# A per-channel normalisation on one core: units of twice the size, with rows of 64 KB

## The chip, the cores and the metric

The kernel runs on one core of one Trainium2 chip. The metric is the device time of one execution in microseconds; the number given for a kernel is the median of its runs. A profile comes from one further execution. Its times are counted from the start of its span, which is a little shorter than the device time.

## What is computed

```python
def setup_inputs():
    B, G, C_per_g, H, W = 4, 8, 16, 256, 256
    return {
        "x": np.random.randn(B, G, C_per_g, H, W).astype(np.float32),
        "gamma": np.random.randn(G, C_per_g).astype(np.float32),
    }

def reference(x, gamma):
    mu = x.mean(axis=(3, 4), keepdims=True)
    var = ((x - mu) ** 2).mean(axis=(3, 4), keepdims=True)
    x_norm = (x - mu) / np.sqrt(var + 1e-5)
    return x_norm * gamma[None, :, :, None, None]
```

There are 4 x 8 x 16 = 512 channels of 256 x 256 = 65,536 float32 values. Each channel is brought to mean zero and variance one, and multiplied by its gamma, of which there are 128 (one for each g and c, the same for all four b). The input is 134.2 MB, and so is the output. Each is moved once.

## The kernel before

A channel lies on 8 partitions, as 8 rows of 8192 values (32 KB). So 128 partitions hold 16 channels, and this is one unit: a tile of 128 x 8192 float32, 4 MB. There are U = 32 units. Six slots (`AHEAD`) hold them in SBUF, and unit u uses slot u % 6.

The order of the work is written out by hand. SP's queue issues the loads, except those of units 1 and 3, which ScalarE's queue issues at the start. ScalarE's queue issues all stores. Six loads are issued at once; after that the load of unit u + 6 (L48) waits until unit u has been normalised and stored, since it overwrites its slot.

For each unit:

- VectorE sums each row (`reduce_sum`, L102), and ScalarE sums the squares of each row (`Square` with `accum_out`, L103). Both read the whole tile at the same time.
- One matmul (L113) with the matrix `navg` adds up the 8 rows of each channel, for the sum and the sum of squares together, and leaves the negative means in `ps` on every row of the channel. `navg` holds -1/65536 in 8 x 8 blocks along the diagonal.
- VectorE makes the negative variance (`nvar`, L114), ScalarE its root (`std`, L118), VectorE the reciprocal (L122) and the product with gamma (`scale`, L124).
- VectorE normalises the whole tile in place (L127): add the negative mean, multiply by `scale`.
- ScalarE's queue stores the tile (L131), and SP's queue issues the load that comes into this slot next.

`g_col` holds gamma by partition, one column for each of the 8 groups of 16 channels. It is made by `gamma_columns` (L78 to L89): a copy on VectorE that repeats each gamma 8 times in one row, 8 matmuls that turn rows into columns, and a copy out of PSUM. It runs after the first unit's sums. Gamma itself comes on SP's queue, behind the load of unit 0. The table for Sqrt is loaded when the first root is due.

Of the kernel before, what the change touches and what calls it, by code (L numbers as in the profile page):

```python
# [1 line left out]

# [4 lines left out]

F32 = mybir.dt.float32
U8 = mybir.dt.uint8
ALU = mybir.AluOpType  # L10
ACTF = mybir.ActivationFunctionType
AX = mybir.AxisListType


@with_exitstack
def kernel(
    ctx: ExitStack,
    tc: tile.TileContext,
    x: bass.AP,
    gamma: bass.AP,  # L20
    out: bass.AP,
):
    nc = tc.nc
    B, G, C, H, W = x.shape
    P = nc.NUM_PARTITIONS
    HW = H * W
    n_ch = B * G * C
    S = 8
    K = P // S
    F = HW // S  # L30
    U = n_ch // K
    NG = (G * C) // K
    AHEAD = 6
    assert HW % S == 0 and (G * C) % K == 0

    xv = x.rearrange("b g c h w -> (b g c h w)").rearrange("(u p f) -> u p f", p=P, f=F)
    ov = out.rearrange("b g c h w -> (b g c h w)").rearrange("(u p f) -> u p f", p=P, f=F)
    gv = gamma.rearrange("g c -> (g c)")

    data = ctx.enter_context(tc.tile_pool(name="data", bufs=1))  # L40
    singles = ctx.enter_context(tc.tile_pool(name="singles", bufs=1))
    psum = ctx.enter_context(tc.tile_pool(name="psum", bufs=4, space=bass.MemoryType.PSUM))
    ctx.enter_context(tc.manual_schedule())

    slots = [data.tile([P, F], F32, name=f"xt{i}") for i in range(AHEAD)]

    def load(u, queue):
        queue.dma_start(out=slots[u % AHEAD][:], in_=xv[u])  # L48


    g_row = singles.tile([1, G * C], F32, name="g_row")
    for u in range(AHEAD):
        load(u, nc.scalar if u in (1, 3) else nc.sync)
        if u == 1:
            nc.sync.dma_start(out=g_row[:], in_=gv[None, :])


    eps_t = singles.tile([P, 1], F32, name="eps_t")
    nc.gpsimd.memset(eps_t[:], 1e-5)
    one = singles.tile([1, 1], F32, name="one")  # L60
    nc.gpsimd.memset(one[:], 1.0)
    navg = singles.tile([P, K, S], F32, name="navg")
    nc.gpsimd.memset(navg[:], -1.0 / HW)  # L63
    nc.gpsimd.affine_select(  # L64
        out=navg[:], in_=navg[:], pattern=[[-S, K], [0, S]], compare_op=ALU.is_ge,
        fill=0.0, base=0, channel_multiplier=1,
    )
    nc.gpsimd.affine_select(  # L68
        out=navg[:], in_=navg[:], pattern=[[S, K], [0, S]], compare_op=ALU.is_ge,
        fill=0.0, base=S - 1, channel_multiplier=-1,  # L70
    )
    navg_w = navg[:].rearrange("p k s -> p (k s)")
    g_rep = singles.tile([1, NG, K, S], F32, name="g_rep")
    g_ps = psum.tile([P, NG], F32, name="g_ps", bufs=1)
    g_col = singles.tile([P, NG], F32, name="g_col")

    def gamma_columns():
        nc.vector.tensor_copy(  # L78
            out=g_rep[:],
            in_=g_row[:].rearrange("o (n k) -> o n k", n=NG).unsqueeze(3).to_broadcast([1, NG, K, S]),  # L80
        )
        for n in range(NG):
            nc.tensor.matmul(  # L83
                out=g_ps[:, n : n + 1],
                lhsT=g_rep[:, n].rearrange("o k s -> o (k s)"),
                rhs=one[:],
                start=True, stop=True,
            )
        nc.vector.tensor_copy(out=g_col[:], in_=g_ps[:])  # L89

    junk = singles.tile([P, F], U8, name="junk")

    st = singles.tile([P, U, 2], F32, name="st")
    nvar = singles.tile([P, U], F32, name="nvar")
    std = singles.tile([P, U], F32, name="std")
    rstd = singles.tile([P, U], F32, name="rstd")
    scale = singles.tile([P, U], F32, name="scale")

    squares = []
    for u in range(U):  # L100
        t = slots[u % AHEAD]
        nc.vector.reduce_sum(out=st[:, u, 0:1], in_=t[:], axis=AX.X)  # L102
        square = nc.scalar.activation(  # L103
            out=junk[:], in_=t[:], func=ACTF.Square, accum_out=st[:, u, 1:2],
        )
        if u:

            tc.declare_no_dep(square.ins, squares[-1].ins, reason="junk, ordered by the root between")
        squares.append(square)
        if u == 0:  # L110
            gamma_columns()
        ps = psum.tile([P, 2], F32, name="ps")
        nc.tensor.matmul(out=ps[:], lhsT=navg_w, rhs=st[:, u], start=True, stop=True)  # L113
        nc.vector.tensor_scalar(  # L114
            out=nvar[:, u : u + 1], in0=ps[:, 0:1], scalar1=ps[:, 0:1],
            scalar2=ps[:, 1:2], op0=ALU.mult, op1=ALU.add,
        )
        nc.scalar.activation(  # L118
            out=std[:, u : u + 1], in_=nvar[:, u : u + 1], func=ACTF.Sqrt,
            bias=eps_t[:], scale=-1.0,  # L120
        )
        nc.vector.reciprocal(out=rstd[:, u : u + 1], in_=std[:, u : u + 1])  # L122
        g = u % NG
        nc.vector.tensor_mul(  # L124
            out=scale[:, u : u + 1], in0=rstd[:, u : u + 1], in1=g_col[:, g : g + 1],
        )
        nc.vector.tensor_scalar(  # L127
            out=t[:], in0=t[:], scalar1=ps[:, 0:1], scalar2=scale[:, u : u + 1],
            op0=ALU.add, op1=ALU.mult,
        )  # L130
        nc.scalar.dma_start(out=ov[u], in_=t[:])  # L131
        if u + AHEAD < U:
            load(u + AHEAD, nc.sync)


# [1 line left out]
_INS = ['x', 'gamma']  # L137
_OUTS = [((4, 8, 16, 256, 256), 'float32')]


# [23 lines left out]
```

## Time and profile before

| what | value |
|---|---|
| median of 9 runs | 627.1 us (626.81 to 627.25) |
| profiled execution | 627.1 us, its span 625.4 us |
| VectorE busy | 442.9 us, 71% of the span |
| ScalarE busy | 239.9 us, 38% |
| TensorE busy (matmul) | 21.4 us, 3% |
| HBM read and written | 134.22 MB each, 429 GB/s over the span |
| the queue DMA q10 (all stores and two loads) | 4896 packets, 142.61 MB, 52.8% of the 16 engines' span |
| the queue DMA q1 (30 loads and gamma) | 4322 packets, 125.83 MB, 46.8% |

The share of a queue is the time that its packets took, against the span of all 16 DMA engines; the two together fill it. SP, the queue that issues loads, waited 538.9 us in all for stores to end, in 26 waits: a load cannot be issued until the store has emptied its slot. A packet in the trace is one descriptor: here one row of 32 KB, or the 4 bytes that count up a semaphore at the end of a transfer.

### The profile page before, as it was taken

How to read it: one execution, taken by the hardware profiler on the slowest of the kernel's cores; microseconds unless marked ns; L12 is line 12 of the kernel's file. 1: busy time of each engine (PE TensorE's matmuls, PEld its weight loads, DVE VectorE, ACT ScalarE, POOL GpSimd, SP SyncE). 2: the span in 40 equal slices, each digit the busy share in tenths (PEclk: the TensorE clock that was granted, in tenths of full speed). 3: DMA queues.
4: the chain of work that ended last, by engine and by line, in shares of the span. 5: the costliest groups of instructions: out<-in, count | busy, mean ns of one | idle time of the engine just before them, and what ended most of it. 6: DMA issues, size and time to landing. Idle time of an engine off the chain costs nothing.

```text
span 625.4 us, 628 instructions
## 1 busy us (share of the span) xinstructions
PE 21.4 (3%) x80; PEld 19.5 (3%) x80; DVE 442.9 (71%) x162; ACT 239.9 (38%) x98; POOL 1.3 (0%) x9
## 2 busy tenths in 40 slices
PE   0020000000000000000000000000000000000000
PEld 0020000000000000000000000000000000000000
DVE  0569999999898667867668676686766877667710
ACT  0435555544444423444224442244432444323400
POOL 0000000000000000000000000000000000000000
DMA  8999999999999999999999999999999999999998
GB/s 369 436 434 405 436 436 436 436 436 436 434 434 428 428 428 432 436 434 436 436 436 434 436 432 432 430 430 428 436 436 434 436 436 432 436 436 434 430 425 361
DMA packets 9220, 268.46 MB, mean 429 GB/s; under 512 B 1025, under 2 KB 1026, under 8 KB 1026
## 3 DMA queue, kind: packets, MB, share of 16 engines
q10 hardware_dynamic: 4896, 142.61, 52.8%
q1 hardware_dynamic: 4322, 125.83, 46.8%
q14 instruction: 2, 0.02, 0.0%
HBM read 134.22 MB, written 134.22 MB: 429 GB/s over the span
## 4 chain that ended last, share of the span: by engine, by line
DMA 62%; DVE 30%; PE 2%; issue 1%; ACT 1%; SPq 0%; ACTq 0%
DMA xt<-in_x_dram 54%; DVE st L102 24%; DMA out_dram<-xt 7%; DVE xt L127 5%; PE ps L113 2%; DVE nvar L114 1%; PE g_ps L83 1%; ACT std L118 0%; ACT L118 0%; DVE rstd L122 0%; DVE scale L124 0%; DVE g_rep L78 0%; SPq L48 0%; ACTq L118 0%
## 5 line engine op out<-in xcount | busy, mean ns | idle before, releaser
L102 DVE TENSOR_REDUCE st<-xt 128x1 f32<-128x8192 f32 x32 | 277.9, 8684 | 110.5 <-DMA xt<-in_x_dram 110.5
L103 ACT ACTIVATE junk<-xt 128x8192 uint8<-128x8192 f32 x32 | 225.0, 7030 | 266.4 <-DMA xt<-in_x_dram 212.4
L127 DVE TENSOR_SCALAR xt<-xt,ps,scale 128x8192 f32<-128x8192 f32 x32 | 145.6, 4550 | 1.2
L118 ACT ACTIVATE std<-nvar,eps_t 128x1 f32<-128x1 f32 x32 | 9.4, 295 | 76.0 <-DVE nvar L114 76.0
L113 PE MATMUL ps<-st,navg 128*128 128x2 f32 x64 | 17.9, 349 | 536.7 <-DVE st L102 536.7
L113 PEld LDWEIGHTS ps<-st,navg 128*128 128x128 f32 x64 | 16.1, 312 | 538.4 <-issue 538.4
L114 DVE TENSOR_SCALAR nvar<-ps 128x1 f32<-128x1 f32 x32 | 9.2, 286 | 23.4 <-PE ps L113 23.4
L122 DVE RECIPROCAL rstd<-std 128x1 f32<-128x1 f32 x32 | 5.2, 164 | 12.9 <-ACT std L118 12.9
L103 ACT ACTIVATION_READ_ACCUMULATOR junk<-xt 128x1 f32 x32 | 6.0, 186 | 0.0
L124 DVE TENSOR_TENSOR scale<-rstd,g_col 128x1 f32<-128x1 f32 x32 | 5.1, 159 | 1.1
L83 PE MATMUL g_ps<-one,g_rep 1*128 1x1 f32 x16 | 3.5, 346 | 32.1 <-DVE g_rep L78 32.1
L83 PEld LDWEIGHTS g_ps<-one,g_rep 1*128 1x128 f32 x16 | 3.5, 325 | 32.0 <-issue 32.0
L118 ACT ACT_TABLE_LOAD x1 | 1.3, 1283 | 6.8 <-DVE nvar L114 6.8
L89 DVE COPY g_col<-g_ps 128x8 f32<-128x8 f32 x1 | 0.2, 167 | 3.7 <-PE g_ps L83 3.7
L103 ACT ACT_TABLE_LOAD x1 | 1.3, 1283 | 1.7 <-PEq L148 1.7
L78 DVE COPY g_rep<-g_row 1x1024 f32<-1x1024 f32 x1 | 0.7, 671 | 0.0
L64 POOL TENSOR_SCALAR_AFFINE_SELECT navg<-navg 128x128 f32<-128x128 f32 x1 | 0.4, 405 | 0.1
L68 POOL TENSOR_SCALAR_AFFINE_SELECT navg<-navg 128x128 f32<-128x128 f32 x1 | 0.4, 399 | 0.1
L63 POOL MEMSET navg<- 128x128 f32 x1 | 0.2, 222 | 0.0
L148 POOL MEMSET const-bfloat16-1.0<- 128x1 bf16 x1 | 0.1, 102 | 0.0
L148 POOL MEMSET const-uint8-127<- 128x1 uint8 x1 | 0.1, 102 | 0.0
L148 POOL MEMSET const-float32-0.0<- 128x1 f32 x1 | 0.1, 99 | 0.3 <-issue 0.3
(3 smaller groups left out, 0.3 us busy)
## 6 DMA issues: line engine op xcount, KB each, us to landing
out_dram<-xt ACTq DMA_DIRECT2D x32, 4096.0 KB, 64.4
xt<-in_x_dram SPq DMA_DIRECT2D x30, 4096.0 KB, 29.0
xt<-in_x_dram ACTq DMA_DIRECT2D x2, 4096.0 KB, 31.5
g_row<-in_gamma_dram SPq DMA_DIRECT2D x1, 0.5 KB
```

The source lines that it names most:

```text
L64: nc.gpsimd.affine_select(out=navg[:], in_=navg[:], pattern=[[-S, K], [0, S]], compare_op=ALU.is_ge, fill=0.0, base=0, channel_multiplier=1,)
L68: nc.gpsimd.affine_select(out=navg[:], in_=navg[:], pattern=[[S, K], [0, S]], compare_op=ALU.is_ge, fill=0.0, base=S - 1, channel_multipli ...
L78: nc.vector.tensor_copy(out=g_rep[:], in_=g_row[:].rearrange("o (n k) -> o n k", n=NG).unsqueeze(3).to_broadcast([1, NG, K, S]),)
L83: nc.tensor.matmul(out=g_ps[:, n : n + 1], lhsT=g_rep[:, n].rearrange("o k s -> o (k s)"), rhs=one[:], start=True, stop=True,)
L102: nc.vector.reduce_sum(out=st[:, u, 0:1], in_=t[:], axis=AX.X)
L103: square = nc.scalar.activation(out=junk[:], in_=t[:], func=ACTF.Square, accum_out=st[:, u, 1:2],)
L113: nc.tensor.matmul(out=ps[:], lhsT=navg_w, rhs=st[:, u], start=True, stop=True)
L114: nc.vector.tensor_scalar(out=nvar[:, u : u + 1], in0=ps[:, 0:1], scalar1=ps[:, 0:1], scalar2=ps[:, 1:2], op0=ALU.mult, op1=ALU.add,)
L118: nc.scalar.activation(out=std[:, u : u + 1], in_=nvar[:, u : u + 1], func=ACTF.Sqrt, bias=eps_t[:], scale=-1.0,)
L122: nc.vector.reciprocal(out=rstd[:, u : u + 1], in_=std[:, u : u + 1])
L124: nc.vector.tensor_mul(out=scale[:, u : u + 1], in0=rstd[:, u : u + 1], in1=g_col[:, g : g + 1],)
L127: nc.vector.tensor_scalar(out=t[:], in0=t[:], scalar1=ps[:, 0:1], scalar2=scale[:, u : u + 1], op0=ALU.add, op1=ALU.mult,)
```

## The change

A unit becomes 32 channels. A channel now lies on 4 partitions, as rows of 16,384 values (64 KB); a slot holds 128 x 16384 float32, 8 MB, and there are 3 of them (`SL`). V = 16 such units cover the input. In the listing, v counts units, h the two halves of a unit (16 channels, 64 rows each). Half h lies on every second partition, from partition h on (`t[h::2]`). Each half is loaded by one transfer and stored by another.

- The last unit keeps the old form: two narrow units of 16 channels, 8 partitions for each, side by side in the columns of one slot, each with its own load (L57 of the new listing; wide halves are loaded on L59) and store over all 128 partitions, and with its own sums.
- All loads are on SP's queue. Gamma comes first on ScalarE's queue. The gamma columns (two for the last two narrow units, four for the wide ones) are made ahead of all units, and a Sqrt of `eps_t`, whose result isn't used, loads the table ahead too.
- The matrix for wide units, `navg_w`, is made by GpSimd: within a block of 8 partitions, -1/65536 where the row and the column number differ by an even number. `navg_n` for the narrow ones is the old matrix.
- In a wide unit the squares come in two instructions of 8192 columns, with one accumulator each, and the matmul becomes three: one for the sum, two that add up the squares.
- VectorE normalises the first 10,240 columns (`DV`) of a wide unit. ScalarE normalises the other 6,144 with `Identity`, with `scale` and a `shift` (negative mean times `scale`), which is one more small VectorE instruction.

```diff
-    S = 8
-    AHEAD = 6
+    SL = 3
+    FW = HW // 4
+    FN = HW // 8
+    V = n_ch // 32
+    DV = 10240
+    xw = xf.rearrange("(v h r f) -> v h r f", h=2, r=P // 2, f=FW)
+    ow = of.rearrange("(v h r f) -> v h r f", h=2, r=P // 2, f=FW)
+    xn = xf.rearrange("(n p f) -> n p f", p=P, f=FN)
+    on = of.rearrange("(n p f) -> n p f", p=P, f=FN)
-    slots = [data.tile([P, F], F32, name=f"xt{i}") for i in range(AHEAD)]
-    def load(u, queue):
-        queue.dma_start(out=slots[u % AHEAD][:], in_=xv[u])
+    slots = [data.tile([P, FW], F32, name=f"xt{i}") for i in range(SL)]
+    def load_slot(v):
+        t = slots[v % SL]
+        for h in range(2):
+            if v == V - 1:
+                nc.sync.dma_start(out=t[:, h * FN : (h + 1) * FN], in_=xn[2 * v + h])
+            else:
+                nc.sync.dma_start(out=t[h::2], in_=xw[v, h])
...
-    for u in range(AHEAD):
-        load(u, nc.scalar if u in (1, 3) else nc.sync)
-        if u == 1:
-            nc.sync.dma_start(out=g_row[:], in_=gv[None, :])
+    nc.scalar.dma_start(out=g_row[:], in_=gv[None, :])
+    for v in range(SL):
+        load_slot(v)
...
+    nc.scalar.activation(out=root_eps[:], in_=eps_t[:], func=ACTF.Sqrt)
...
+    for d in (-6, -4, -2, 0, 2, 4, 6):
+        nc.gpsimd.affine_select(
+            out=navg_w[:], in_=navg_w[:], pattern=[[-8, P // 8], [-1, 8]],
+            compare_op=ALU.not_equal, fill=-1.0 / HW, base=-d, channel_multiplier=1,
+        )
+    block8(navg_w)
...
+    def unit(i, t, width, navg, g):
+        nsq = width // FN
+        nc.vector.reduce_sum(out=st[:, i, 0:1], in_=t, axis=AX.X)
+        for k in range(nsq):
+            sq = nc.scalar.activation(
+                out=junk[:], in_=t[:, k * FN : (k + 1) * FN], func=ACTF.Square,
+                accum_out=st[:, i, 1 + k : 2 + k],
+            )
...
+        if nsq == 1:
+            nc.tensor.matmul(out=ps[:], lhsT=w, rhs=st[:, i, 0:2], start=True, stop=True)
+        else:
+            nc.tensor.matmul(out=ps[:, 0:1], lhsT=w, rhs=st[:, i, 0:1], start=True, stop=True)
+            nc.tensor.matmul(out=ps[:, 1:2], lhsT=w, rhs=st[:, i, 1:2], start=True, stop=False)
+            nc.tensor.matmul(out=ps[:, 1:2], lhsT=w, rhs=st[:, i, 2:3], start=False, stop=True)
...
+        w = width
+        if nsq > 1:
+            w = DV
+            nc.vector.tensor_mul(out=shift, in0=ps[:, 0:1], in1=scale)
+            nc.scalar.activation(
+                out=t[:, w:], in_=t[:, w:], func=ACTF.Identity, bias=shift, scale=scale,
+            )
         nc.vector.tensor_scalar(
+            out=t[:, :w], in0=t[:, :w], scalar1=ps[:, 0:1], scalar2=scale,
             op0=ALU.add, op1=ALU.mult,
         )
...
+    for v in range(V):
+        t = slots[v % SL]
+        if v == V - 1:
+            for h in range(2):
+                part = t[:, h * FN : (h + 1) * FN]
+                unit(i, part, FN, navg_n, h)
+                nc.scalar.dma_start(out=on[2 * v + h], in_=part)
+                i += 1
+        else:
+            unit(i, t[:], FW, navg_w, NE + v % NW)
+            for h in range(2):
+                nc.scalar.dma_start(out=ow[v, h], in_=t[h::2])
+            i += 1
+        if v + SL < V:
+            load_slot(v + SL)
```

## The prediction

> **What bounds the kernel now.** I read the page's slices first, then its groups and DMA issues, then the timeline of the end, then the trace's packet records (one per descriptor: queue, start, duration, bytes).
>
> ```profile
> span 625.4 us, 628 instructions
> DVE  0569999999898667867668676686766877667710
> ACT  0435555544444423444224442244432444323400
> DMA  8999999999999999999999999999999999999998
> GB/s 369 436 434 405 436 436 436 436 436 436 434 434 428 428 428 432 436 434 436 436 436 434 436 432 432 430 430 428 436 436 434 436 436 432 436 436 434 430 425 361
> L102 DVE TENSOR_REDUCE st<-xt 128x1 f32<-128x8192 f32 x32 | 277.9, 8684 | 110.5 <-DMA xt<-in_x_dram 110.5
> L103 ACT ACTIVATE junk<-xt 128x8192 uint8<-128x8192 f32 x32 | 225.0, 7030 | 266.4 <-DMA xt<-in_x_dram 212.4
> L127 DVE TENSOR_SCALAR xt<-xt,ps,scale 128x8192 f32<-128x8192 f32 x32 | 145.6, 4550 | 1.2
> out_dram<-xt ACTq DMA_DIRECT2D x32, 4096.0 KB, 64.4
> xt<-in_x_dram SPq DMA_DIRECT2D x30, 4096.0 KB, 29.0
> ```
>
> The DMA row is full from end to end: the 16 DMA engines bound everything, and VectorE's 71% is not the limit. A store takes 64.4 us from issue to landing, a load 29.0: stores stand in a long queue. Now the end:
>
> ```profile
> 561.33 8.69 DVE L102 TENSOR_REDUCE st<-xt 128x1 f32<-128x8192 f32 x1 [4.34 <-DMA xt<-in_x_dram]
> 571.80 4.55 DVE L127 TENSOR_SCALAR xt<-xt,ps,scale 128x8192 f32<-128x8192 f32 x1
> 580.70 7.03 ACT L103 ACTIVATE junk<-xt 128x8192 uint8<-128x8192 f32 x1 [9.31 <-DMA xt<-in_x_dram]
> 580.70 8.69 DVE L102 TENSOR_REDUCE st<-xt 128x1 f32<-128x8192 f32 x1 [4.34 <-DMA xt<-in_x_dram]
> 591.17 4.55 DVE L127 TENSOR_SCALAR xt<-xt,ps,scale 128x8192 f32<-128x8192 f32 x1
> 595.75 0.34 ACTq L131 DMA_DIRECT2D out_dram<-xt  x1
> ```
>
> Units come every 19.37 us (580.70 less 561.33). From the last landing, reduce to store issue takes 15.05 us (580.70 to 595.75), all of it under stores queued earlier: those run to 623.9 by the packet records, and the span ends at 625.4.
>
> The records give more. First packet at 1.8 us, last end 623.9, so 622.1 us of transfer. A 32 KB packet starts 1.2097 us after the one before on its engine. Load and store packets alternate one for one, whatever the queues hold, and a transfer's 4-byte semaphore packet also takes a turn. A load's last packet ended 1.6 us before the reduce (579.11, 580.70). Issue to first packet is 1.0 us on idle engines (0.8 to 1.8), but 5.0 us for the first store (43.11 to 48.1), which enters while loads run and costs 0.9 us.
>
> [...]
>
> **The change, part by part.** The sum is on the profiled execution: 627.1 us, span 625.4 plus 1.7 around it; the median is 627.1 too.
>
> Start. The copy for gamma (0.67 us), its 16 matrix passes (3.54) and the Sqrt table (1.28) leave the stretch from 31.2 to 37.8 us and go beside the first landing (22.6 us). POOL's masks grow by some ten instructions of 0.2 to 0.4 us, done by about 7 us; the first matmul wants them near 40. Gamma is one 512-byte packet ahead on ScalarE's queue; SP now issues all early loads, six at 0.35 us, against 9.7 us of transfer each. Value of all this: 0. Loads alone fill the engines to 1.8 + 6 x 9.66 = 59.8 us, and the first store is ready at 22.7 + 25.1 = 48 (43 before). Without this cover each late microsecond would count.
>
> Compute of a wide unit: reduce 2 x 8.68 = 17.4; three matmuls, 0.7 to 1.7 (one is 0.57 with its two passes); nvar, root, reciprocal, scale 1.0 with gaps; shift 0.2 by the scale row; normalise 4.55 x 10240/8192 = 5.7. About 25.1 us against 38.6 us of DMA per unit. Beside it ScalarE does two squares, 14.4, and 6144 columns of Identity: 5.3 at Square's rate, at worst twice that. Both ends are hidden: a slot turns in 3 x 38.6 = 116 us, less load 39, landing and compute 28, first store half 19 and refill 3 to 5, leaving some 25 us in the store queue. The stores' extra waits on shared DMA semaphores (half h of unit v waits for half h of v-2, with the next squares behind it on ScalarE) end some 12 us before the issue. Cost 0.
>
> Packets. [...] Fifteen units go from 16 to 8 packets per engine each way: 240 fewer, 240 x 5 ns = **-1.2 us**. If rows were cut in two again, 0[...].
>
> The end. This decides. A wide load waits for its own half's store alone. The two narrow loads of the last unit (L57) write all 128 partitions, so both wait for both stores of unit 12, on SP with nothing behind them. So the load queue runs dry while unit 12's second store moves, and stores run ahead. Count turns from that store's end. Stores of units 13 and 14 hold 4 halves x (4 packets + 1 semaphore) = 20 turns, then the first narrow store 9. The two loads hold 18. They arrive 1.6 + 1.0 = 2.6 us later at best, 6.6 with the first store's 5.0: two or three store packets of 2.41 us are gone. The other 17 or 18 store turns pair off with the 18 load turns. But a store turn is 64 KB and a load turn 32 KB: stores get 63% of the engines. When the last load ends, units 13 and 14 are out and only the first narrow store is left: 8 x 1.21 = 9.7 us. The last half needs 1.6 landing + 15.05 + 1.0 to its first packet = 17.7. The engines stand idle 17.7 - 9.7 = **+8.0 us**. One store turn more or less gives 5.6 to 10.4; a restart stall as at the first store 0.9 on top. Before, 623.9 - 579.1 = 44.8 us remained after the last load, less 9.7 of its own store: nothing was exposed.
>
> Sum: 627.1 - 1.2 + 8.0 = 633.9, say **634.0 us**; this case's own range is 631.5 to 638.
>
> **Rivals.**
> [...]
>
> Equal shares at the end, not slower. If engines share by bytes and not by descriptors, the last loads' 19.4 us go beside 19.4 of stores. From unit 12's end 48.3 us of stores remain; head start 5 to 7, so 22 to 24 are left when the loads end, more than 17.7. No idle time: 627.1 - 1.2 = 625.9. It decides below a store share of about 56%: then at most 48.3 - 17.7 = 30.6 us of stores are gone. Against: strict alternation of records; all were of one size, so before can't tell.
>
> The change doesn't do what it says: 64 KB rows are moved as two of 32 KB. Then turns are equal, no packet is saved, no idle: 627.1. For it: before shows nothing over 32 KB.
>
> **How the numbers follow.** Forecast 0.57, collisions 0.19, cut rows 0.13, equal shares 0.11. A measurement here tells about 0.2% (1.25 us) from no change. 625.9 stands on that edge, so half of its chance is faster: 0.06. Same: 0.13 + 0.05 = 0.18. Slower: 0.57 + 0.19 = 0.76. The range leaves out the collisions: 625.5 to 638, with 0.81 inside.
>
> **What would show it.** Right: packets of 65,536 bytes at about 2.41 us; full DMA slices until some 611 us, then about 8 us without packets while one narrow reduce, chain and normalise run; the last store issued near 619; the last loads half as dense in packets' time as the stores beside them. Wrong: packets still of 32 KB; packet durations well over 2.41 us all through (collisions); no DMA gap, with over 17.7 us of stores after the last load; or idle time in the middle, which would mean the 25 us in the store queue don't exist.

## The result, and the profile after

| | median | executions | ratio, 95% interval |
|---|---|---|---|
| before | 627.1 us | 626.8 to 627.5 (29) | |
| changed | 639.4 us | 637.3 to 642.3 (9) | 1.0199 [1.0189, 1.0209] |
| forecast | 634.0 us | range 625.5 to 638.0 | |

Slower, as forecast, but by 12.3 us and not by 6.9, and past the upper end of the range by 1.4. The changed kernel also scatters over 5.0 us, the kernel before over 0.7. The profiled execution is the fastest of the nine, 637.3 us with a span of 635.4: it stands 10.2 us above the one before, and is read with that in mind.

First the page of the changed kernel: its slices, groups (busy us and mean ns of one behind the first bar) and DMA issues (the last number is the median us from issue to landing).

```profile
span 635.4 us, 657 instructions
...
DMA  9999999999999999999999999999999999999976
GB/s 396 396 462 396 458 400 458 417 441 454 408 450 409 450 421 437 454 417 446 413 446 433 429 454 417 441 421 437 450 417 447 425 433 437 410 421 406 421 309 264
DMA packets 5381, 268.47 MB, mean 422 GB/s; under 512 B 1025, under 2 KB 1026, under 8 KB 1026
...
L129 DVE TENSOR_REDUCE st<-xt 128x1 f32<-128x16384 f32 (+1 forms) x17 | 275.7, 16215 | 205.7 <-DMA xt<-in_x_dram 205.7
...
L162 DVE TENSOR_SCALAR xt<-xt,ps,cf 128x10240 f32<-128x10240 f32 (+1 forms) x17 | 93.2, 5484 | 0.1
L159 ACT ACTIVATE xt<-xt,cf 128x6144 f32<-128x6144 f32 x15 | 82.6, 5508 | 10.2 <-DVE cf L158 10.2
...
xt<-in_x_dram SPq DMA_DIRECT2D x30, 26.1
out_dram<-xt ACTq DMA_DIRECT2D x30, 45.5
```

The DMA row is as full as before in 38 slices, and thins out in the last two (309 and 264 GB/s, against 425 and 361 before). VectorE still waits 205.7 us for loads, so it is not the limit. The GB/s row swings between 396 and 462: a slice is 15.9 us, and 6 packets of 64 KB on each of 16 engines make 396 GB/s in it, 7 make 462. By itself the swing is no loss.

Next the timeline of the changed kernel's end: start, us, engine and line, and in brackets the idle time before and who ended it.

```profile
542.67 17.22 DVE L129 TENSOR_REDUCE st<-xt 128x1 f32<-128x16384 f32 x1 [13.35 <-DMA xt<-in_x_dram]
547.56 1.03 SPq L57 DMA_DIRECT2D xt<-in_x_dram  x2
...
579.31 8.69 DVE L129 TENSOR_REDUCE st<-xt 128x1 f32<-128x8192 f32 x1 [11.16 <-DMA xt<-in_x_dram]
...
594.37 0.38 ACTq L174 DMA_DIRECT2D out_dram<-xt  x1
...
608.05 8.69 DVE L129 TENSOR_REDUCE st<-xt 128x1 f32<-128x8192 f32 x1 [13.71 <-DMA xt<-in_x_dram]
...
618.52 4.55 DVE L162 TENSOR_SCALAR xt<-xt,ps,cf 128x8192 f32<-128x8192 f32 x1
623.10 0.34 ACTq L174 DMA_DIRECT2D out_dram<-xt  x1
```

Both narrow loads (L57) are issued together at 547.56, after unit 12's stores. The second lands at 608.05, and its store is issued at 623.10, 15.05 us later, the same 15.05 as before. What the engines do meanwhile stands in the windows (window, us, busy time of PE, PEld, DVE, ACT and POOL, granted clock, DMA share, GB/s):

```profile
605.00:610.00 5.00, 0.00 (x0) 0.00 (x0) 1.95 (x1) 1.95 (x1) 0.00 (x0) 1.00 0.88 380
610.00:615.00 5.00, 0.00 (x0) 0.00 (x0) 5.00 (x1) 5.00 (x2) 0.00 (x0) 1.00 0.93 400
615.00:620.00 5.00, 0.56 (x2) 0.50 (x2) 3.82 (x5) 0.47 (x3) 0.00 (x0) 1.00 0.17 72
620.00:625.00 5.00, 0.00 (x0) 0.00 (x0) 3.07 (x1) 0.00 (x0) 0.00 (x0) 1.00 0.24 105
625.00:630.00 5.00, 0.00 (x0) 0.00 (x0) 0.00 (x0) 0.00 (x0) 0.00 (x0) 1.00 0.98 419
```

Between 615 and 625 the DMA engines are four fifths idle, while VectorE and ScalarE work on the last narrow unit. The packet records put the gap at 6.7 to 9.7 us on each engine, 7.8 in the mean. (The records carry no engine number; a packet is put on the engine whose last packet ended just before it, which gives 16 chains.) This is how the gap came about on one engine (start in us; L load, S store, n a narrow unit's 32 KB, all others 64 KB; in brackets ns above the usual duration):

```
S542.4 S544.8 S547.2 S549.7 Ln552.1 S553.3 Ln555.7 Ln556.9 S558.1 Ln560.5 S561.7[+441] Ln564.6
S565.8[+247] Ln568.5 S569.7 Ln572.1 Ln573.3[+454] S575.0 S577.4 Ln579.8 S581.0 Ln583.4 S584.6
... Ln595.9 S597.1[+368] Ln599.9 S601.1[+31] Ln603.5 Sn604.7 Sn605.9 Sn607.1 Sn608.4 ...
```

From 544.8 three store packets run alone, until the narrow load arrives. From 552 on a load of 32 KB (1.21 us) and a store of 64 KB (2.42 us) take turns, so stores get two thirds of the time. Two of a kind in a row are places where the other queue's turn went to a 4-byte semaphore packet (9 ns). When the last load ends, only the first narrow store is left (Sn). So a turn was one descriptor here, of 32 KB or of 64.

The gap alone doesn't fill the account. 64 KB packets take 2,418 ns in the median and start 2.414 us apart: the usual packet is as cheap as forecast (2.41). But some last longer, up to 3.8 us. I call a packet stretched if it lasts over 30 ns more than the usual one, and add up the excess:

| | stretched packets | excess per engine | idle at the end | first packet later | sum against before | measured (last packet's end) |
|---|---|---|---|---|---|---|
| before | 48 of 8192 | 1.4 us | 0 | | | 623.9 |
| changed | 213 of 4352 | 4.8 | 7.8 us | 0.3 us | -1.2 + 3.4 + 7.8 + 0.3 = 10.3 | 633.8 (+9.9) |
| changed, once more (e0) | 447 of 4352 | 8.7 | 8.0 | 0.4 | -1.2 + 7.3 + 8.0 + 0.4 = 14.5 | 637.9 (+14.0) |

The -1.2 us are 240 packets fewer per engine at 5 ns each. In the forecast these 5 ns were my estimate; the starts show them: two packets of 32 KB less one of 64 KB leave 5 ns (2 x 1.2097 - 2.414 us).

So the difference consists of the gap that was forecast and of stretched packets, which were not in the sum; and the 4 us between two executions are stretched packets, not a longer gap.

The place of the stretched packets matters too. Of the 3.4 us more than before, the profiled execution has 2.6 after 540 us, where the narrow loads of 128 rows go beside wide stores of 64 rows, and only 0.4 between 120 and 540 us. In e0 it is 3.0 after 540 us and 3.5 between: the end is much alike in both, and most of what differs lies in the middle.

### The profile page after: what moved, and what is told of

It is laid out like the page before. It is cut to its first block, busy times and chain, and to the rows that moved or that the text cites. A ratio compares the mean times of both kernels' runs of the same rounds, so it can differ in the third digit from the quotient of the medians.

```text
span 635.4 us, 657 instructions
## 1 busy us (share of the span) xinstructions
PE 25.4 (4%) x106; PEld 24.0 (4%) x106; DVE 381.6 (60%) x107; ACT 317.0 (50%) x98; POOL 5.1 (1%) x19
## 2 busy tenths in 40 slices
DMA packets 5381, 268.47 MB, mean 422 GB/s; under 512 B 1025, under 2 KB 1026, under 8 KB 1026
## 4 chain that ended last, share of the span: by engine, by line
DMA 50%; DVE 23%; another core or an unknown queue 19%; ACT 4%; PE 2%; SPq 1%; issue 0%; DVEq 0%; ACTq 0%
DMA out_dram<-xt 29%; DMA xt<-in_x_dram 21%; DVE st L129 19%; ACT xt L159 3%; DVE xt L162 3%; PE ps L144 1%; SPq L59 0%; PE ps L146 0%; PE ps L145 0%; ACT cf L152 0%; DVE cf L148 0%; DVE cf L153 0%; DVE cf L154 0%; PE ps L142 0%
## 5 line engine op out<-in xcount | busy, mean ns | idle before, releaser
L129 DVE TENSOR_REDUCE st<-xt 128x1 f32<-128x16384 f32 (+1 forms) x17 | 275.7, 16215 | 205.7 <-DMA xt<-in_x_dram 205.7
L162 DVE TENSOR_SCALAR xt<-xt,ps,cf 128x10240 f32<-128x10240 f32 (+1 forms) x17 | 93.2, 5484 | 0.1
L159 ACT ACTIVATE xt<-xt,cf 128x6144 f32<-128x6144 f32 x15 | 82.6, 5508 | 10.2 <-DVE cf L158 10.2
L152 ACT ACTIVATE cf<-cf,eps_t 128x1 f32<-128x1 f32 x17 | 5.0, 294 | 74.4 <-DVE cf L148 74.4
L144 PE MATMUL ps<-st,navg_w 128*128 128x1 f32 x30 | 8.8, 362 | 534.7 <-DVE st L129 534.7
L144 PEld LDWEIGHTS ps<-st,navg_w 128*128 128x128 f32 x30 | 7.5, 312 | 536.0 <-DVE st L129 500.3
L148 DVE TENSOR_SCALAR cf<-ps 128x1 f32<-128x1 f32 x17 | 4.9, 286 | 24.6 <-PE ps L146 23.1
L145 PE MATMUL ps<-st,navg_w 128*128 128x1 f32 x30 | 8.5, 352 | 0.0
L146 PE MATMUL ps<-st,navg_w 128*128 128x1 f32 x30 | 8.5, 352 | 0.0
L145 PEld LDWEIGHTS ps<-st,navg_w 128*128 128x128 f32 x30 | 8.2, 334 | 0.0
L146 PEld LDWEIGHTS ps<-st,navg_w 128*128 128x128 f32 x30 | 8.2, 333 | 0.0
L153 DVE RECIPROCAL cf<-cf 128x1 f32<-128x1 f32 x17 | 2.8, 164 | 6.2 <-ACT cf L152 6.2
L154 DVE TENSOR_TENSOR cf<-cf,g_col 128x1 f32<-128x1 f32 x17 | 2.7, 159 | 0.6
L91 POOL TENSOR_SCALAR_AFFINE_SELECT navg_w<-navg_w 128x128 f32<-128x128 f32 x7 | 2.9, 413 | 0.5
## 6 DMA issues: line engine op xcount, KB each, us to landing
xt<-in_x_dram SPq DMA_DIRECT2D x30, 26.1
```

Of the source, the lines that this page charges most:

```text
L91: nc.gpsimd.affine_select(out=navg_w[:], in_=navg_w[:], pattern=[[-8, P // 8], [-1, 8]], compare_op=ALU.not_equal, fill=-1.0 / HW, base=-d ...
L129: nc.vector.reduce_sum(out=st[:, i, 0:1], in_=t, axis=AX.X)
L144: nc.tensor.matmul(out=ps[:, 0:1], lhsT=w, rhs=st[:, i, 0:1], start=True, stop=True)
L145: nc.tensor.matmul(out=ps[:, 1:2], lhsT=w, rhs=st[:, i, 1:2], start=True, stop=False)
L146: nc.tensor.matmul(out=ps[:, 1:2], lhsT=w, rhs=st[:, i, 2:3], start=False, stop=True)
L148: nc.vector.tensor_scalar(out=nvar, in0=ps[:, 0:1], scalar1=ps[:, 0:1], scalar2=ps[:, 1:2], op0=ALU.mult, op1=ALU.add,)
```

## The experiments

Every kernel is an edit of the changed one, unless it says otherwise. They ran beside the kernel before, whose median was 627.0 to 627.1 each time. "Gap" is the idle time at the end.

**e0: the changed kernel once more**, without an edit, for its scatter.

> The changed kernel once more, unedited, for a second profile and more times, since its nine runs spread over 5 us (637.3 to 642.3) and the profiled one was the fastest. Theory (turns at the end): the steady part is the same to 0.5 us in both profiles, and the difference between two executions lies between the landing of the last load and the first packet of the last store: a gap of 7 to 13 us, in steps of a store turn (2.4 us) or half of one. Rival (64-row transfers collide now and then): the gap is again near 8 us, and packets of 64 KB take longer than 2.42 us in many places of the middle.

Measured: 641.8 us (637.9 to 642.7), ratio 1.0223 [1.0185, 1.026]. Its profile is of an execution of 641.4 us. The gap is 8.0 us on average, as in the shorter execution. Between 120 and 540 us, far from both ends, 256 of 2761 packets of 64 KB last longer than 2.45 us, 251 of them loads; in the shorter execution there are 48. So what was written down as the rival held: the gap stays near 8 us, and the scatter comes from the middle.

**e1: the store of unit 14 in four column transfers**, each 64 rows of 32 KB, so that its turns are as long as the narrow loads' turns.

```diff
-            for h in range(2):
-                nc.scalar.dma_start(out=ow[v, h], in_=t[h::2])
+            if v == V - 2:
+                for c in range(2):
+                    for h in range(2):
+                        nc.scalar.dma_start(
+                            out=ow[v, h][:, c * FN : (c + 1) * FN],
+                            in_=t[h::2, c * FN : (c + 1) * FN],
+                        )
+            else:
...
```

> Only unit 14's store is cut: four transfers of 64 rows x 32 KB in place of two of 64 rows x 64 KB. The wait of the last unit's loads for both stores of unit 12 stays. Theory (a store turn of 64 KB against a load turn of 32 KB starves the last loads): with equal turns over unit 14's store, some 12 turns of it and the 9.7 us of the first narrow store are left when the last load ends, more than the 17.7 us needed: no gap, 626 to 628 us. Rival (the late start of the last loads alone costs the time, turns do nothing): unchanged, 637 to 642 us, gap 8 us or more.

Measured: 631.6 us (630.0 to 634.4), ratio 1.0078 [1.0051, 1.0105]. The timeline of e1:

```profile
599.82 8.69 DVE L129 TENSOR_REDUCE st<-xt 128x1 f32<-128x8192 f32 x1 [3.31 <-DMA xt<-in_x_dram]
...
614.88 0.34 ACTq L174 DMA_DIRECT2D out_dram<-xt  x1
```

and its windows:

```profile
615.00:620.00 5.00, 0.00 (x0) 0.00 (x0) 0.00 (x0) 0.00 (x0) 0.00 (x0) 1.00 0.99 426
620.00:625.00 5.00, 0.00 (x0) 0.00 (x0) 0.00 (x0) 0.00 (x0) 0.00 (x0) 1.00 0.99 426
625.00:630.00 5.00, 0.00 (x0) 0.00 (x0) 0.00 (x0) 0.00 (x0) 0.00 (x0) 1.00 0.24 105
```

The same bytes are left to move, and the same two loads wait for the same two stores. Only the turns have another length: the last load lands 8.2 us earlier (599.82 against 608.05), and the DMA share between 615 and 620 goes from 0.17 to 0.99. The gap by turns is shown. But 4.6 us above the kernel before remain, where none was expected. In its packet records 226 packets are stretched, 5.6 us per engine, and the engines end between 625.5 and 628.3 us (before: 622.9 to 623.9).

**e2: the store of unit 12 by columns**, so that each narrow load waits for one half of the columns instead of for the whole unit. The edit is that of e1 with `v == V - 1 - SL`.

> Only unit 12's store is changed: by columns, four transfers of 64 rows x 32 KB, the first two of the left 8192 columns. So the first load of the last unit waits for half of that store only, and its second load for the other half. Turns stay unequal beside units 13 and 14. Theory (late start and unequal turns together): the loads start some 10 us earlier, so 8 to 10 us more of stores are left when they end: gap 0 to 2 us, 626 to 629 us. Rival (unequal turns alone make the gap, whenever the loads start): gap 5 us or more, 633 to 640 us.

Measured: 634.9 us (632.1 to 638.5), ratio 1.0129 [1.0089, 1.0169]. The timeline of e2:

```profile
600.69 8.69 DVE L129 TENSOR_REDUCE st<-xt 128x1 f32<-128x8192 f32 x1 [14.97 <-DMA xt<-in_x_dram]
...
615.74 0.34 ACTq L174 DMA_DIRECT2D out_dram<-xt  x1
```

An earlier load closes the gap too, as expected: the packet records show none at the end. So the gap needs both, late loads and unequal turns. The time was missed by 6 us, and e2 is slower than e1: 371 packets are stretched, 7.5 us per engine, and the engines end between 627.1 and 632.2 us. The slowest engine sets the end of the transfer here: it is done 3.5 us after the mean of all (632.2 against 628.7).

**e3: the last unit is wide like the others**, with its own halves' waits and equal turns (`if False:` in place of `if v == V - 1:`, in the load and in the loop).

> The last unit is wide like the others: 64-row transfers of 64 KB rows, each load waits for its own half of unit 12's store, turns are equal. Its compute takes 25 us and not 15 from the last landing. Theory: the last load ends with one to one and a half halves of unit 13's and all of unit 14's store left, 24 to 27 us, against 1.6 + 25.4 + 1.0 = 28 us needed: a gap of 1 to 4 us, 627 to 630 us. Rival (any last unit exposes most of its compute in this kernel with three slots): a gap of 10 us or more, 636 us or more.

Measured: 634.8 us (631.4 to 641.1), ratio 1.0107 [1.0079, 1.0136]. Missed by 5 us. The profile fell on the longest of its executions, 641.1 us, so its gap is the largest that I can show and not the usual one. The timeline of e3:

```profile
561.25 0.47 SPq L59 DMA_DIRECT2D xt<-in_x_dram  x1
...
591.52 17.22 DVE L129 TENSOR_REDUCE st<-xt 128x1 f32<-128x16384 f32 x1 [15.16 <-DMA xt<-in_x_dram]
...
617.11 1.13 ACTq L179 DMA_DIRECT2D out_dram<-xt  x2
```

A wide unit takes 25.6 us from landing to the store's issue, not 15.05, and the stores before it are out at 603 to 608 us on fifteen engines. These idle 9.8 to 15.3 us; the last one, which stretched packets had put about 12 us behind, idles 3.0 (its stores end at 615.2). The slowest engine sets the end of a load here too: on fifteen engines the last load's data is in by 584.1, on this one at 588.7, and the reduce starts at 591.52.

**e4: the halves on 64 neighbouring partitions**, with the matrix to match. The rows of HBM that a transfer moves are those of the changed kernel; only where they lie in SBUF is another.

```diff
-                nc.sync.dma_start(out=t[h::2], in_=xw[v, h])
+                nc.sync.dma_start(out=t[h * 64 : (h + 1) * 64], in_=xw[v, h])
...
-                nc.scalar.dma_start(out=ow[v, h], in_=t[h::2])
+                nc.scalar.dma_start(out=ow[v, h], in_=t[h * 64 : (h + 1) * 64])
```

> The halves of a wide unit lie on 64 neighbouring partitions in place of every second one (a channel on four neighbours, matrix and gamma columns made for that). Theory[...] 64 KB packets take 3.6 to 4.8 us[...], 900 to 1240 us. Rival[...]: 2.4 us a packet, 636 to 642 us.

Measured: 894.5 us, in one execution. The slices of e4:

```profile
span 892.7 us, 643 instructions
...
GB/s 197 226 188 282 288 282 294 311 320 308 314 326 317 332 318 291 332 329 341 341 317 308 323 317 311 314 300 314 332 314 341 324 302 297 288 289 363 258 276 206
```

The rate never comes near the 436 of before (363 at most), and the usual packet lasts 3.08 us (2.42 in the changed kernel). The 3.6 to 4.8 us expected of a packet were my estimate, and no run shows them. The placement costs much: 894.5 us are 1.40 times the changed kernel's time and 1.43 times that of before. That it can make packets longer is shown; by what, is not, nor that it does so in the changed kernel, where rows lie on every second partition.

**e5 and e6: unit 0 too as two narrow units**, so that the first store comes sooner and the load queue is longer; e6 with the edit of e1 as well. I had seen stretched packets at the seams between load halves and took an almost empty load queue for the cause.

```diff
-            if v == V - 1:
+            if v in (0, V - 1):
                 nc.sync.dma_start(out=t[:, h * FN : (h + 1) * FN], in_=xn[2 * v + h])
...
-        if v == V - 1:
+        if v in (0, V - 1):
```

> Unit 0 too is split into two narrow units like the last one; the end stays as it is. Both loads of unit 3 then wait for both narrow stores of unit 0 and are issued together, so that every later load is issued some 20 us before the one ahead of it ends (1 to 4 us in the changed kernel, 8 us in the kernel before). Theory (load packets are stretched where the load queue is nearly dry, and this varies from run to run): no stretched load packets between 120 and 540 us, spread of the runs about 1 us; the end still has late loads and unequal turns, gap 0 to 5 us: 627 to 633 us. Rival[...]: stretched packets as often as before, spread 4 us or more.

> Unit 0 narrow, and unit 14's store in four transfers of 32 KB rows. Theory (a nearly dry load queue and unequal turns at the end are all that costs time): no stretched packets in the middle, no gap at the end, 626 to 628.5 us with a spread of 1 us, at best 1 us below the kernel before by its fewer packets. Rival (collisions): 629 to 634 us with a spread of 4 us, as with unit 14 cut alone.

Measured: e5 631.1, 710.0, 731.9 and 733.4 us in four executions; e6 697.3 in the median (637.3 to 709.3). No ratio is given, since one kernel has two speeds. That theory fell: the loads were early (in e5 a wide load landed 45.4 us after its issue in the median, 26.1 in the changed kernel), and the time rose to as much as 94 us above the changed kernel's median. The profile of e5 fell on its shortest execution, with 271 stretched packets, 6.3 us per engine, and no gap. Its end is built like the changed kernel's, but unit 14's loads run until 550 us there, so stores get little head start over the narrow loads. The slices of e6:

```profile
span 707.6 us, 666 instructions
...
GB/s 385 415 430 443 409 437 433 415 452 433 411 426 445 419 404 411 370 378 374 378 359 359 333 356 382 270 367 389 282 374 341 304 367 326 359 356 393 424 319 246
```

and two windows of e6:

```profile
200.00:240.00 40.00, 1.44 (x6) 1.35 (x6) 23.52 (x6) 20.05 (x6) 0.00 (x0) 1.00 1.03 438
400.00:440.00 40.00, 0.00 (x0) 0.00 (x0) 15.44 (x5) 14.91 (x4) 0.00 (x0) 1.00 0.93 352
```

At 200 us the kernel runs at full rate; at 400 it moves 352 GB/s with the engines 93% busy. So in this stretch slow packets are the larger part of the loss, and waiting is the smaller. The records of this stretch show how: two engines start packets at the same times (403.4, 406.4, 409.5, 412.5 and 415.7 us), each 0.5 to 0.9 us too long, while some others keep to 2.42 us. In these packets the two stay in step and are stretched alike. Whether they share something, and what, is not shown. Over the whole execution 1374 packets are stretched, 47 us per engine; another 34 us per engine is idle time, nearly all of it after 400 us. That engines wait there for stores that a stretched engine holds up is likely, but not shown.

**e7 and e10: the 64-row transfers, but with each row in two descriptors of 32 KB** (a slot of 2 x 8200 columns keeps them apart); e10 with the narrow unit first.

```diff
-    slots = [data.tile([P, FW], F32, name=f"xt{i}") for i in range(SL)]
+    slots = [data.tile([P, 2, FN + 8], F32, name=f"xt{i}") for i in range(SL)]
...
-                nc.sync.dma_start(out=t[h::2], in_=xw[v, h])
+                nc.sync.dma_start(
+                    out=t[h::2, :, :FN], in_=xw[v, h].rearrange("r (c f) -> r c f", c=2)
+                )
```

> All else as in the changed kernel, but each 64 KB row lies in SBUF as two pieces of 32 KB with 32 bytes between them, so that every data packet is 32 KB; transfers, waits and units stay, reductions and normalisations read the two pieces in one instruction. Theory (turns, and packets that are long against the lead of the load queue): equal turns everywhere, no gap at the end, little stretching since a turn is half as long: 627 to 629 us, 1.2 us of it for the 240 packets more. Rival (64-row transfers as such are slow, whatever the packet): 631 us or more with stretched packets.

> The kernel with rows in two pieces (32 KB packets in 64-row transfers), and unit 0 narrow as well, which in the 64 KB form took the time to 631 to 733 us. [...] 627.5 to 629 us, no stretched packets. If[...] only the steps were lucky: above 640 us in some runs.

Measured: e7 628.1 us (627.8 to 628.7), ratio 1.0016 [1.001, 1.0023]; e10 666.2 (657.2 to 667.9), ratio 1.0544 [1.0472, 1.0617]. The slices of e7:

```profile
span 626.2 us, 656 instructions
...
GB/s 368 435 433 404 435 435 431 435 435 429 427 427 434 433 433 435 435 434 435 433 435 435 431 435 435 429 427 429 433 435 431 434 435 435 435 433 435 435 429 347
DMA packets 9221, 268.47 MB, mean 429 GB/s; under 512 B 1025, under 2 KB 1026, under 8 KB 1026
```

With all turns of one size and 9221 packets in place of 5381, nearly the whole loss is gone: no gap, 68 stretched packets, 1.6 us per engine. So units of twice the size, the new compute and the new waits cost about 1 us together; in this order of transfers the loss comes with rows of 64 KB. e10 warns against taking this for a cure: 64-row transfers of 32 KB can be stretched as well (823 packets, 24 us per engine).

**e8, e9, e11 and e12: one transfer of all 128 rows per unit and direction**, each channel on four neighbouring partitions. e9 and e11 have the edit of e1 for these rows, e11 and e12 the narrow unit first, e12 rows in two.

```diff
-                nc.sync.dma_start(out=t[h::2], in_=xw[v, h])
+                if h == 0:
+                    nc.sync.dma_start(out=t[:], in_=xa[v])
...
-            for h in range(2):
-                nc.scalar.dma_start(out=ow[v, h], in_=t[h::2])
+            nc.scalar.dma_start(out=oa[v], in_=t[:])
```

> A wide unit is loaded and stored by one transfer of 128 rows x 64 KB instead of two of 64 (a channel on four neighbouring partitions); packets stay at 64 KB, the end stays. Theory[...]: no stretched packets in the middle, runs within 1 us of each other apart from the end's gap of 0 to 5 us: 626 to 631 us. Rival (64 KB packets themselves stretch, by HBM or by a load queue that runs dry): stretched packets stay, spread 4 us or more, 632 us or more.

> As the run before, and unit 14's store goes by columns in two transfers of 128 rows x 32 KB, which makes turns equal at the end. Theory: neither stretching nor a gap, 625.5 to 627.5 us, about 1 us under the kernel before by 240 packets fewer per engine. Rival: as there, 630 us or more.

> Unit 0 narrow and unit 14's store cut, as in the run that gave 637 to 709 us, but wide units go by one transfer of 128 rows x 64 KB. Theory[...]: 625.5 to 628.5 us in every run, no stretched packets. Rival (the narrow first unit or 64 KB packets bring the slowness, whatever the transfers): 637 to 709 us again.

> Narrow first unit, wide units by one transfer of 128 rows, and each row in two pieces of 32 KB: the fourth corner beside 64 rows x 64 KB (637 to 709 us), 64 rows x 32 KB (657 to 668) and 128 rows x 64 KB (630 to 633). Theory (both the 64-row transfers and, less, the 64 KB packets let engines stretch each other's packets): 627 to 628.5 us, runs within 1 us, engines end within 1 us of each other. Rival (with 128 rows the 3 to 6 us left come from the three slots or the ends, not from the packets): 630 to 633 us again.

Measured: e8 633.2 us, 1.0115 [1.0074, 1.0157]; e9 631.5, 1.0084 [1.0052, 1.0116]; e11 632.3, 1.0078 [1.0063, 1.0093]; e12 629.5, 1.0039 [1.0023, 1.0054]. e8 still has a gap (6.1 us in the mean), which comes from its slowest engines: eight have their last load by 583.5 us, just when unit 14's store begins to move; one that is some 5 us late still has five narrow loads to go then, takes turns with that store, and has its last load at 600.9. After 540 us e8 has 0.2 us of stretched packets per engine, the changed kernel 2.6: both have narrow loads beside wide stores there, but e8's stores have 128 rows like the loads. e9 has no gap. Its last two engines are a pair, stretched by 5 us each at the same times, and end at 627.8 and 628.4, while ten others are done by 623.3. With the narrow unit first, the four kernels make a table:

| rows of a transfer | 64 KB descriptors | 32 KB descriptors |
|---|---|---|
| 64 | e6: 697.3 (637.3 to 709.3) | e10: 666.2 (657.2 to 667.9) |
| 128 | e11: 632.3 (630.4 to 632.7) | e12: 629.5 (629.3 to 630.0) |

128 rows take the collapse away in both columns. That edit also halves the number of transfers, makes a load wait for the whole store of its slot, and moves the rows to other partitions; these are not told apart. 32 KB descriptors lower the time clearly in the lower row; in the upper one the ranges overlap. e8 missed what was expected by 2 us, e9 and e11 by some 4, e12 by 1: 64 KB rows keep a rest even with 128 of them.

**e13: the kernel before with only the new start**: gamma first on ScalarE's queue, all loads on SP's, columns and table ahead.

```diff
+    nc.scalar.dma_start(out=g_row[:], in_=gv[None, :])
...
-        load(u, nc.scalar if u in (1, 3) else nc.sync)
-        if u == 1:
-            nc.sync.dma_start(out=g_row[:], in_=gv[None, :])
+        load(u, nc.sync)
...
+    nc.scalar.activation(out=root_eps[:], in_=eps_t[:], func=ACTF.Sqrt)
...
+    gamma_columns()
```

> The kernel before with the start of the change alone: gamma first on ScalarE's queue, all loads on SP's queue, gamma's columns and the Sqrt table ahead of the first unit. Theory of the prediction (all hidden, since loads alone fill the engines until the first store): within 0.5 us of before. Rival (the earlier first store, or one queue for the first loads, moves the whole transfer): 1 us or more either way.

Measured: 627.5 us (627.1 to 629.6), ratio 1.001 [1.0003, 1.0016]. The first store of the kernel before, and then the timeline of e13:

```profile
43.12 0.35 ACTq L131 DMA_DIRECT2D out_dram<-xt  x1
```

```profile
13.21 8.69 DVE L104 TENSOR_REDUCE st<-xt 128x1 f32<-128x8192 f32 x1 [6.58 <-DMA xt<-in_x_dram]
...
28.26 0.38 ACTq L131 DMA_DIRECT2D out_dram<-xt  x1
```

The first store is issued 15 us sooner (28.26 against 43.12), and nothing is gained: in the kernel before the DMA engines were full in this stretch already (a share of 0.97 to 1.01 between 4 and 40 us).

## Why the prediction was half right

- *Start, 0.* Right: e13 measured +0.5 us [0.2, 1.0] (the interval of the ratio times 627), so there is no gain, and at most a small loss. The first store of the changed kernel went out at 49.02 us, forecast 48.
- *Compute, 0.* Right: reduce 17.22 us (17.4 in the sum), normalise 5.61 (5.7), Identity 5.5 (5.3), from landing to store 25.6 (25.1), and no idle time in the middle. e7, which has all of it, bounds its cost at about 1 us.
- *The end, +8.0.* Right, by mechanism and size: 7.8 us in the profile, 8.0 in e0, three store packets alone and then one for one. e1 took it away by the length of the turns alone, e2 by the start of the loads alone. It came later than forecast (last store issued at 623.10, forecast near 619). The rival of equal shares by bytes (no gap) is refuted by the same two, and that of cut rows by 3840 packets of 65,536 bytes.
- *Packets, -1.2.* This step failed. The packet's own 5 ns were right (2 x 1.2097 - 2.414 us), but the step took every packet for a usual one. Stretched packets add 3.4 us per engine in the profiled execution and 7.3 in e0, so that the term measured +2.2 and +6.1 in place of -1.2. For the median, 12.3 less the gap of 7.8 and the later first packet of 0.3 leaves about +4.2, an estimate. The forecast had longer packets only as a rival for the whole run (collisions, at 0.19), all or nothing, with bounds of 0 to 622 us that were my estimate. They were a partial cost beside the gap, in both executions that were profiled.
- *The range.* It let a restart stall of 0.9 us stand on top of the gap, and put all collisions outside. One term of 3 to 7 us inside would have moved the forecast to 637 to 641, and the range with it.
- *Collisions.* What the forecast held against them was my estimate, which no run had shown, and it was no protection for 64-row transfers: with the narrow unit first, the profiles of e6 and e10 have stretched packets of 47 and 24 us per engine, and with 128 rows the time falls from 697.3 and 666.2 us to 632.3 and 629.5 (e11, e12). Which rows an engine took, and what stretches its packets, the runs don't show.

What stays open: the records show which packets are long, not which rows an engine took, so whether the cause of a pair in step lies in SBUF, in HBM or elsewhere is not settled (e11 changes both sides). Nor is it known why e6, with a narrow first unit, has such a pair, why 64-row stores beside 128-row loads come with stretched packets at the end (2.6 us per engine, against 0.2 in e8), and why 64 KB rows cost some 3 us more than 32 KB rows with 128-row transfers (632.3 against 629.5 us).

No version here beat the kernel before.

## What to carry to other kernels

Where two queues drain together, count turns and not bytes: here, with rows of unequal size, the queue with the longer descriptors ran ahead, and the other's last transfer came late (608.05 us, against 599.82 with equal turns in e1). Price stretched packets (3.4 and 7.3 us per engine here) as a part of the sum with a size of its own, not as a rival that happens or doesn't, and let the slowest of the 16 engines set the end (in e2 it ended 3.5 us after the mean). On full DMA engines, rows of equal size in transfers over all partitions were the steady form here (e12 spreads over 0.7 us, as the kernel before does in the first table). One transfer of 128 rows rather than two of 64 on alternate partitions took 632.3 us against 697.3 here (e11, e6).

## What was not expected of the hardware

- One kernel, e5, ran at 631 us in one execution and at 710 to 733 in three, with no change of code.
- In e6, a pair of engines stayed in step for packet after packet, most of them stretched by 0.5 to 0.9 us, beside engines at full speed.
- Loads carry most of the stretching: 76% of the excess time in the changed kernel, 83% in e0, 93% in e2.
